# Holding a tile's pre-norm root and scalings behind the next tile's post-norm sums, at the seam of two layers

## The chip, the core and the metric

The kernel runs on one core of a Trainium2 chip. The metric is device time in microseconds of one execution; lower is better. Engines: PE (TensorE, matmuls), DVE (VectorE), ACT (ScalarE), POOL (GpSimd) and SP (SyncE, which here issues the DMAs). Each engine works through its own instructions in a fixed order and waits where an operand, or a buffer to write to, isn't ready.

## What is computed

Two layers of a decoder on 512 tokens of width 1024, each with a normalisation before its projections and one behind them. Cut to what matters here:

```python
def rms_norm(x, g):
    y = xf * lax.rsqrt(jnp.mean(xf * xf, axis=-1, keepdims=True) + NORM_EPS)
    return y * g

def hybrid_layer(x, w_in, w_out, g_pre, g_post, lb, g_head, sinks):
    h = rms_norm(x, g_pre)
    proj = jnp.einsum('bsd,de->bse', h, w_in)
    ...
    y = jnp.einsum('bse,ed->bsd', jnp.concatenate([o_h, o_a], axis=-1), w_out)
    return x + rms_norm(y, g_post)
```

The seam is the end of layer 0 and the start of layer 1: the last output projection, the post-norm with its residual, the pre-norm of layer 1, and layer 1's first projection (keys and values).

## The kernel before

Tokens are worked in four tiles of 128 (t0 to t3), each with two column halves of 512. To keep fp32 accuracy an operand is split into a high and a low part (`whi`, `wlo` for weights, `hhi`, `hlo` for the normalised input), and a product is three matmuls: high by high, high by low, low by high.

A projection is a queue of units (`Unit`); each unit is one output tile in one of three PSUM banks `pj`, and two units at most are worked at a time, in alternation. `step` issues the three matmuls of one k-slice (L293), then runs what `later` has put off by a number of steps, then converts weights that fall due (L181 on ACT, L182 on DVE or POOL). A weight piece may not be converted past `state["limit"]`, which the seam sets for the first slab of the next layer and lifts after the last tile's pre-norm.

At the seam the following happens for each tile t, all called from `final` as the output units end:

- the unit's result is added to `y` (L887, DVE, reads `pj`), half by half, and each half is squared with its sum (L929, ACT, into `ss`);
- the first half is multiplied by the post-norm gain on POOL (L931), the second on DVE (L936);
- post-norm root: the sum of the two halves (L352, DVE) and the power -0.5 (L354, POOL);
- residual: x plus the scaled y, half by half (L943, DVE, tile `a`, loaded by L920 into one of two buffers), stored to `x_mid` (L944, SP);
- `pre_norm`: squares of the new x (L386, ACT), pre-norm root (again L352 and L354), and the scalings to `xn`, half by half (L401, DVE; their gain lies in PSUM banks `ac`);
- put off by `DEFER` steps, for each half: four transposes into one of three PSUM banks `sc` (L406, PE), the high part (L410, ACT) and the low part (L414, DVE). The low part is the last reader of its `sc` bank.

The units of layer 1's key and value projection need the high and low parts of their tile. They are 24 matmuls of 128x256 each: eight high by high, eight high by low weight, eight low by high.

What stands where on an engine is decided by a scheduler of the language, which is free to move an instruction ahead of others; instructions given to `pin` keep the order in which the program issues them among themselves. In the kernel before, none of the DVE instructions of `final` and of `pre_norm` is pinned.

Of the kernel before, what the change touches and what calls it, by code (L numbers as in the profile page):

```python
# [14 lines left out]
ALU = mybir.AluOpType  # L15
# [5 lines left out]
NT = SEQ // 128  # L21
# [8 lines left out]
QA, IV, FQ, ZA, ZH = 0, 2, 4, 8, 10  # L30
# [10 lines left out]
DEFER = 18  # L41
# [29 lines left out]
def hybrid_kernel(ctx: ExitStack, tc: tile.TileContext, x, wkv, win, wout, g_pre, g_post, lbp, ghead, sinks,  # L71
                  gcol_c, cos_f, sin_f, cos_t, sin_t, masks_c, out):
    nc = tc.nc
# [10 lines left out]
    def pin(ins):  # L84
        return tc.keep_in_program_order(ins)
# [12 lines left out]
    def ac():  # L98
        ac_turn[0] += 1
        return ac_tiles[ac_turn[0] % len(ac_tiles)]  # L100

    def tmp(tag, dt=F32, n=1):

        t = tp.tile([P, n, 512] if n > 1 else [P, 512], dt, tag=tag, name=tag, bufs=TB[tag])
        return t
# [10 lines left out]
    slab_first = {}  # L116
# [37 lines left out]
    state = {"raw": 0, "conv": 0, "limit": KT // 2}  # L154
# [47 lines left out]
    def later(steps, key, fn):  # L202

        waiting.append([steps, key, fn])
# [131 lines left out]
    hT = {}  # L336
# [12 lines left out]
    def rstd2(ss, keep=lambda ins: ins):  # L349

        t = sm.tile([P, 1], F32, tag="s1", name="s1")
        keep(nc.vector.scalar_tensor_tensor(t, ss[:, 0:1], EPS, ss[:, 1:2], op0=ALU.add, op1=ALU.add))  # L352
        r = sm.tile([P, 1], F32, tag="r1", name="r1")
        keep(nc.gpsimd.tensor_tensor(r, t, mhalf[:, 0:1], op=ALU.pow))  # L354
        return r

    def halves(tag):
        t = tmp(tag, n=2)
        return [t[:, 0], t[:, 1]]

    def load_g(g):
        t = halves("b")
        for c in range(2):
            nc.sync.dma_start(t[c], g[c * 512:(c + 1) * 512].partition_broadcast(P))
        return t
# [54 lines left out]
            if self.tt == NT - 1 and c == 1:  # L420
                state["limit"] = None

    def pre_norm(tt, xt, g, hT, key, defer):
        m = Norm(tt, xt, g, hT)
        m.square(0)
        m.square(1)
        m.r = rstd2(m.ss)
        m.scale(0)
        m.scale(1)
        later(defer, None, lambda: m.rest(0))  # L430
        later(defer, key, lambda: m.rest(1))

    def new_hT():
        return (hp.tile([P, KT, SEQ], F32R, tag="hhi", name="hhi"), hp.tile([P, KT, SEQ], F32R, tag="hlo", name="hlo"))


    def layer(l, last):
# [440 lines left out]
        def wo_stream(b, s, final=None):  # L878
            def evac(o, tt, ch, c0, n):
                if (b, s) == ("a", 0):  # L880
                    if ch == 0:
                        yt[tt] = big.tile([P, 2, 512], F32, tag="oy", name="y", bufs=6)
                    nc.scalar.copy(yt[tt][:, ch], o)
                else:
                    y = yt[tt][:, ch, c0:c0 + n]
                    with tc.high_priority(200 if final else 0):
                        nc.vector.tensor_tensor(y, o, y, op=ALU.add)  # L887
                if final is not None:
                    final(tt, ch, c0, n)

            if final:
                todo = [(tt, ch, 0, 512) for tt in range(NT) for ch in range(2)]
                if last:

                    todo[-1:] = [(NT - 1, 1, 0, 256), (NT - 1, 1, 256, 256)]
            else:
                todo = [(tt, ch, 0, 512) for ch in range(2) for tt in range(NT)]
            enqueue(("out", l, f"{b}{s}"),
                    [(range(4 * ch, 4 * ch + 4), lambda k, w, tt=tt: tuple(t[:, k % 4, tt * P:(tt + 1) * P] for t in ops_t[b, s]),
                      lambda k, w, c0=c0, n=n: tuple(t[:, c0:c0 + n] for t in w[k]),  # L900
                      lambda o, e=(tt, ch, c0, n): evac(o, *e), [("o", l, b, s, tt)], n)
                     for tt, ch, c0, n in todo])


        hT2 = {}

        def final(tt, ch, c0, n):
            split = n < 512
            if ch == 0:
                if tt == 0:  # L910
                    hT2["gpost"] = load_g(g_post[l])
                    if not last:
                        hT2["gpre"] = [ac() for _ in range(2)]
                        for c, t in enumerate(load_g(g_pre[l + 1])):
                            nc.scalar.copy(hT2["gpre"][c], t)
                        state["limit"] = slab_first["in", l + 1, QA][0] + 2
                        hT[l + 1] = new_hT()
                hT2["x"] = halves("a")
                for c in range(2):
                    nc.sync.dma_start(hT2["x"][c], (x if l == 0 else x_mid)[tt * P:(tt + 1) * P, c * 512:(c + 1) * 512])  # L920
                hT2["ss"] = sm.tile([P, 2], F32, tag="ss", name="ss")
            xt, ss, y = hT2["x"], hT2["ss"], yt[tt]
            if c0:

                hT2["ss"] = sm.tile([P, 2], F32, tag="ss", name="ss")
                nc.vector.tensor_tensor(hT2["ss"][:, 0:1], ss[:, 0:1], ss[:, 1:2], op=ALU.add)
                ss = hT2["ss"]
            junk = tmp("u")
            nc.scalar.activation(junk[:, 0:n], y[:, ch, c0:c0 + n], AF.Square, scale=1.0 / 32.0, accum_out=ss[:, ch:ch + 1])  # L929
            if ch == 0:  # L930
                nc.gpsimd.tensor_tensor(y[:, 0], y[:, 0], hT2["gpost"][0], op=ALU.mult)  # L931
                return
            if not c0:
                hT2["yg"] = tmp("s")
            yg = hT2["yg"]
            nc.vector.tensor_tensor(yg[:, c0:c0 + n], y[:, 1, c0:c0 + n], hT2["gpost"][1][:, c0:c0 + n], op=ALU.mult)  # L936
            if split and not c0:
                return
            r = rstd2(ss)
            parts = [(0, y[:, 0], 0, 512)] + [(1, yg, e, n) for e in range(0, 512, n)]  # L940
            for i, (c, v, e, w) in enumerate(parts):
                xs = xt[c][:, e:e + w]
                nc.vector.scalar_tensor_tensor(xs, v[:, e:e + w], r, xs, op0=ALU.mult, op1=ALU.add)  # L943
                (nc.scalar if split and i == 1 else nc.sync).dma_start(  # L944
                    (out if last else x_mid)[tt * P:(tt + 1) * P, c * 512 + e:c * 512 + e + w], xs)
            if not last:
                pre_norm(tt, xt, hT2["gpre"], hT[l + 1], ("h", l + 1, tt), DEFER)


        for s_ in ORDER:  # L950
# [51 lines left out]
    gpre = [ac() for _ in range(2)]  # L1002
# [15 lines left out]
    m, n = head[0], head[1]  # L1018
# [146 lines left out]
```

## Time and profile before

| what | us |
|---|---|
| median of three runs | 923.82 |
| fastest, slowest of them | 923.78, 924.04 |
| span of the profiled execution (first to last instruction) | 921.4 |
| chain that ended last, PE's share of it | 88% |
| largest waits of PE in the seam (460 to 478) | 1.01, 1.01, 0.69 |

The profiled execution has no time of its own beside its span; the runs say what an execution takes as a whole. A row of the timeline gives start, duration, engine, line, operation, tile written <- tiles read, shape and count, and in brackets how long the engine stood idle ahead of it and who ended that. A row of the windows gives a stretch, its length, the busy time of PE, PE's weight loads, DVE, ACT and POOL (with counts), the granted clock of PE, the DMA engines' share and GB/s.

### The profile page before, as it was taken

The page shows a single profiled execution, that of the slowest core. Times are in us where ns is not written, and L with a number is a line of the kernel's source. Part 1 is how long each engine was busy: PE and PEld are TensorE (multiplying, and loading weights), DVE is VectorE, ACT ScalarE, POOL GpSimd, SP SyncE. Part 2 cuts the span into 40 slices and gives each one's busy share as a digit, 9 for nine tenths or more (in the row PEclk, how much of TensorE's full clock was granted, in tenths as well). Part 3 has the DMA queues.
Part 4 walks back from the last instruction along what each step waited for, and adds up shares of the span by engine and source line. Part 5 has one row for each costly group of instructions (what it writes and reads, how often), then busy time and mean ns, then how long its engine had stood idle before and what let it go on. Part 6 is the DMA issues. An engine that isn't in the chain of part 4 may idle for free.

```text
span 921.4 us, 19000 instructions
## 1 busy us (share of the span) xinstructions
PE 904.5 (98%) x7240; PEld 752.0 (82%) x7240; DVE 667.3 (72%) x1326; ACT 463.4 (50%) x1100; POOL 272.9 (30%) x292
## 2 busy tenths in 40 slices
PE   8999999999999999999989999999999999999996
PEld 7888887888888888888878878888788888888885
DVE  5967977869854896655786689876889449866556
ACT  6535767652755423534463366686446463245242
POOL 3325443304313142121332254450134022330102
PEclk9999999999999999999999999999999999999999
DMA  6684612333221432334356556222322323213413
GB/s 224 192 231 136 172 36 81 92 93 94 70 85 54 130 91 70 92 106 129 111 164 177 161 147 173 58 69 92 94 70 81 96 77 94 82 47 94 136 35 137
DMA packets 56570, 100.74 MB, mean 109 GB/s; under 512 B 6560, under 2 KB 9120, under 8 KB 56480
## 3 DMA queue, kind: packets, MB, share of 16 engines
q1 hardware_dynamic: 56192, 99.40, 36.6%
q8 instruction: 57, 0.93, 0.4%
q14 instruction: 33, 0.27, 0.1%
q10 hardware_dynamic: 288, 0.14, 0.1%
HBM read 86.93 MB, written 12.58 MB: 108 GB/s over the span
## 4 chain that ended last, share of the span: by engine, by line
PE 88%; DVE 6%; ACT 3%; issue 1%; POOL 1%; DMA 0%; POOLq 0%; DVEq 0%; ACTq 0%
PE pj L293 72%; PE sc L561 2%; PE sc L744 2%; PE ac L614 2%; PE ac L815 2%; DVE wlo L182 1%; PE ac L818 1%; PE ac L802 1%; PE sc L588 1%; ACT s L575 1%; PE sc L867 1%; PE sc L790 1%; POOL r L354 1%; DVE a L943 1%; PE sc L550 0%
## 5 line engine op out<-in xcount | busy, mean ns | idle before, releaser
L182 DVE TENSOR_TENSOR wlo<-raw,whi 128x512 fp32r<-128x512 f32 x249 | 182.9, 748 | 50.0 <-ACT whi L181 49.3
L181 ACT CAST whi<-raw 128x512 fp32r<-128x512 f32 x256 | 154.2, 620 | 106.0 <-PE pj L293 95.2
L293 PE MATMUL pj<-hhi,wlo 128*128 128x512 f32 x512 | 203.8, 398 | 0.0
L293 PE MATMUL pj<-hhi,whi 128*128 128x512 f32 x512 | 199.8, 390 | 0.0
L293 PE MATMUL pj<-hlo,whi 128*128 128x512 f32 x512 | 199.6, 390 | 0.0
L293 PE MATMUL pj<-whi,ops 128*128 128x512 f32 (+1 forms) x520 | 172.5, 394 | 0.0
L293 PEld LDWEIGHTS pj<-hhi,whi 128*128 128x128 f32 x512 | 96.1, 188 | 20.7
L293 PEld LDWEIGHTS pj<-whi,ops 128*128 128x128 f32 x520 | 97.2, 188 | 19.3
L293 PEld LDWEIGHTS pj<-hhi,wlo 128*128 128x128 f32 x512 | 96.1, 188 | 19.3
L293 PEld LDWEIGHTS pj<-hlo,whi 128*128 128x128 f32 x512 | 96.3, 188 | 18.6
L293 PE MATMUL pj<-whi,hlo 128*128 128x512 f32 x256 | 103.6, 405 | 0.0
L293 PE MATMUL pj<-wlo,ops 128*128 128x512 f32 (+1 forms) x260 | 100.8, 388 | 0.0
L293 PE MATMUL pj<-wlo,hhi 128*128 128x512 f32 x256 | 100.5, 392 | 0.3 <-DVE wlo L182 0.2
L293 PE MATMUL pj<-whi,hhi 128*128 128x512 f32 x256 | 100.3, 392 | 0.0
L763 POOL TENSOR_TENSOR k<-k,tot 128x256 f32<-128x256 f32 x80 | 64.2, 831 | 107.2 <-PE sc L744 57.7
L575 ACT ACTIVATE s<-sc,negm 128x128 f32<-128x128 f32 x128 | 45.5, 368 | 38.9 <-DVE negm L569 34.8
L762 DVE TENSOR_TENSOR q<-q,tot 128x256 f32<-128x256 f32 x80 | 48.8, 647 | 12.8 <-PE sc L750 7.0
L293 PEld LDWEIGHTS pj<-whi,hhi 128*128 128x128 f32 x256 | 48.1, 188 | 10.3
L293 PEld LDWEIGHTS pj<-wlo,ops 128*128 128x128 f32 x260 | 49.0, 188 | 8.8
L293 PEld LDWEIGHTS pj<-wlo,hhi 128*128 128x128 f32 x256 | 48.3, 189 | 9.1 <-DVE wlo L182 1.2
L293 PEld LDWEIGHTS pj<-whi,hlo 128*128 128x128 f32 x256 | 48.2, 188 | 8.0
L582 POOL TENSOR_TENSOR s<-s,sums 128x512 f32<-128x512 f32 x32 | 34.1, 1067 | 44.5 <-DVE sums L580 29.2
(188 smaller groups left out, 1416.2 us busy)
## 6 DMA issues: line engine op xcount, KB each, us to landing
raw<-in_win_dram SPq DMA_DIRECT2D x192, 256.0 KB, 2.7
raw<-in_wout_dram SPq DMA_DIRECT2D x64, 256.0 KB, 2.7
stack<-rot SPq DMA_DIRECT2D x16, 512.0 KB, 3.4
qs<-stack SPq DMA_DIRECT2D x32, 256.0 KB, 4.9
a<-in_x_dram SPq DMA_DIRECT2D x12, 256.0 KB, 3.0
raw<-in_wkv_dram SPq DMA_DIRECT2D x8, 256.0 KB, 4.2
x_mid<-a SPq DMA_DIRECT2D x8, 256.0 KB, 2.1
a<-x_mid SPq DMA_DIRECT2D x8, 256.0 KB, 3.2
```

Of the source, the lines that this page charges most:

```text
L181: keep(nc.scalar.copy(hi, v))
L182: keep((nc.gpsimd if i in on_pool and i % 2 else nc.vector).tensor_tensor(lo, v, hi.bitcast(F32), op=ALU.subtract))
L293: nc.tensor.matmul(u.o, lhsT=u.sta(k, u.w)[i], rhs=u.mov(k, u.w)[j], start=(n == 0), stop=(n == len(u.list) - 1))
L354: keep(nc.gpsimd.tensor_tensor(r, t, mhalf[:, 0:1], op=ALU.pow))
L561: pin(nc.tensor.matmul(S[:, h * 256:(h + 1) * 256], lhsT=q[:, 2 * hp_ + h, t_], rhs=kst[v][p][:, (n - 1) * P:(n + 1) * P], start=(h == 0 a ...
L575: nc.scalar.activation(pt[:, h * P:(h + 1) * P], cur[h], AF.Exp, bias=negm[:, h:h + 1], scale=SCALE, accum_out=sums[:, h:h + 1])
L582: nc.gpsimd.tensor_tensor(pv, pv, sums.unsqueeze(2).broadcast_to([P, 4, P]), op=ALU.mult)
L614: pin(nc.tensor.matmul(U, lhsT=vst[v][:, blk, :], rhs=d, start=(i == 0), stop=(i == len(terms) - 1)))
L744: pin(nc.tensor.matmul(L[32 * b:32 * b + 32, c:c + 16], lhsT=k[:, o_:o_ + 32], rhs=qv[:, blk:blk + qu, 1, :], start=True, stop=True, tile_ ...
L762: nc.vector.tensor_tensor(qv[:, :, 1, :], qv[:, :, 1, :], tv[:, :, 0].unsqueeze(2).broadcast_to([P, nb, hh]), op=ALU.mult)
L763: nc.gpsimd.tensor_tensor(kv_[:, :, 0, :], kv_[:, :, 0, :], tv[:, :, 1].unsqueeze(2).broadcast_to([P, nb, hh]), op=ALU.mult)
L815: pin(nc.tensor.matmul(O[:, c], lhsT=A[:, c], rhs=vs(j, n), start=(n == 0), stop=False))
```

## The change

`pre_norm` no longer issues the root and the scalings. It issues the squares and returns two functions, `root` and `scales`. `final` keeps them in `hT2["held"]` and calls them when the next tile has come to its own post-norm: `root` ahead of that tile's post-norm root, `scales` right behind it, with the transposes put off by `DEFER - 8` steps, counted from there. The last tile calls its own at once. Roots, scalings and residuals are pinned. The limit for early weight conversion falls from two pieces to one.

```diff
-    def pre_norm(tt, xt, g, hT, key, defer):
+    def pre_norm(tt, xt, g, hT, key):
         m = Norm(tt, xt, g, hT)
         m.square(0)
         m.square(1)
-        m.r = rstd2(m.ss)
-        m.scale(0)
-        m.scale(1)
-        later(defer, None, lambda: m.rest(0))
-        later(defer, key, lambda: m.rest(1))
+
+        def root():
+            m.r = rstd2(m.ss, pin)
+
+        def scales(defer):
+            for c in range(2):
+                pin(m.scale(c))
+            later(defer, None, lambda: m.rest(0))
+            later(defer, key, lambda: m.rest(1))
+
+        return root, scales
...
-                        state["limit"] = slab_first["in", l + 1, QA][0] + 2
+                        state["limit"] = slab_first["in", l + 1, QA][0] + 1
...
-            r = rstd2(ss)
+            held = hT2.pop("held", None)
+            if held:
+                held[0]()
+            r = rstd2(ss, pin if held else lambda ins: ins)
+            if held:
+                held[1](DEFER - 8)
             parts = [(0, y[:, 0], 0, 512)] + [(1, yg, e, n) for e in range(0, 512, n)]
             for i, (c, v, e, w) in enumerate(parts):
                 xs = xt[c][:, e:e + w]
-                nc.vector.scalar_tensor_tensor(xs, v[:, e:e + w], r, xs, op0=ALU.mult, op1=ALU.add)
+                (pin if not last else lambda ins: ins)(nc.vector.scalar_tensor_tensor(xs, v[:, e:e + w], r, xs, op0=ALU.mult, op1=ALU.add))
...
             if not last:
-                pre_norm(tt, xt, hT2["gpre"], hT[l + 1], ("h", l + 1, tt), DEFER)
+                hT2["held"] = pre_norm(tt, xt, hT2["gpre"], hT[l + 1], ("h", l + 1, tt))
+                if tt == NT - 1:
+                    root, scales = hT2.pop("held")
+                    root()
+                    scales(DEFER)
```

The lines behind the diff are numbered higher by 6 to 11 in the changed kernel: L887 becomes L893, L929 L935, L931 L937, L936 L942, L943 L954. What the scheduler makes of it is shown at three places. A row gives line, operation, tile written <- tiles read, and shape; the numbers tell buffers apart.

First place: DVE behind t0's residual (`a_5128`), where t1's second half is evicted. Before:

```order
L943 SCALAR_TENSOR_TENSOR a_5128<-s_5157,r1_5161,a_5128 128x512
L352 SCALAR_TENSOR_TENSOR s1_5171<-ss_5168 128x1
L887 TENSOR_TENSOR y_3077<-pj_5180,y_3077 128x512
L401 SCALAR_TENSOR_TENSOR xn_5167<-a_5128,r1_5173,ac1_82 128x512
L401 SCALAR_TENSOR_TENSOR xn_5167<-a_5128,r1_5173,ac0_81 128x512
L936 TENSOR_TENSOR s_5214<-y_3077,b_5118 128x512
L352 SCALAR_TENSOR_TENSOR s1_5216<-ss_5194 128x1
L887 TENSOR_TENSOR y_3126<-pj_5201,y_3126 128x512
```

With the change:

```order
L954 SCALAR_TENSOR_TENSOR a_5128<-s_5157,r1_5161,a_5128 128x512
L893 TENSOR_TENSOR y_3077<-pj_5174,y_3077 128x512
L942 TENSOR_TENSOR s_5208<-y_3077,b_5118 128x512
L352 SCALAR_TENSOR_TENSOR s1_5210<-ss_5168 128x1
L352 SCALAR_TENSOR_TENSOR s1_5214<-ss_5188 128x1
L401 SCALAR_TENSOR_TENSOR xn_5167<-a_5128,r1_5212,ac1_82 128x512
L401 SCALAR_TENSOR_TENSOR xn_5167<-a_5128,r1_5212,ac0_81 128x512
L893 TENSOR_TENSOR y_3126<-pj_5195,y_3126 128x512
```

t0's pre-norm sum (`ss_5168`) has moved behind t1's eviction and gain, and stands directly ahead of t1's post-norm sum; the scalings follow both.

Second place: DVE where t1's pre-norm (`ss_5225`, `xn_5224`), t2's residual (`a_5248`, then `a_5242`), t3's evictions (`y_3165`) and t0's low halves (`hlo`) meet. Before:

```order
L352 SCALAR_TENSOR_TENSOR s1_5228<-ss_5225 128x1
L936 TENSOR_TENSOR s_5271<-y_3126,b_5118 128x512
L401 SCALAR_TENSOR_TENSOR xn_5224<-a_5191,r1_5230,ac1_82 128x512
L401 SCALAR_TENSOR_TENSOR xn_5224<-a_5191,r1_5230,ac0_81 128x512
L352 SCALAR_TENSOR_TENSOR s1_5273<-ss_5251 128x1
L414 TENSOR_TENSOR hlo_5127<-sc0_78,hhi_5126 128x4x128
L943 SCALAR_TENSOR_TENSOR a_5248<-y_3126,r1_5275,a_5248 128x512
L887 TENSOR_TENSOR y_3165<-pj_5258,y_3165 128x512
L943 SCALAR_TENSOR_TENSOR a_5248<-s_5271,r1_5275,a_5248 128x512
L414 TENSOR_TENSOR hlo_5127<-sc1_79,hhi_5126 128x4x128
L887 TENSOR_TENSOR y_3165<-pj_5294,y_3165 128x512
```

With the change:

```order
L942 TENSOR_TENSOR s_5265<-y_3126,b_5118 128x512
L352 SCALAR_TENSOR_TENSOR s1_5267<-ss_5225 128x1
L352 SCALAR_TENSOR_TENSOR s1_5271<-ss_5245 128x1
L401 SCALAR_TENSOR_TENSOR xn_5224<-a_5185,r1_5269,ac1_82 128x512
L401 SCALAR_TENSOR_TENSOR xn_5224<-a_5185,r1_5269,ac0_81 128x512
L954 SCALAR_TENSOR_TENSOR a_5242<-y_3126,r1_5273,a_5242 128x512
L893 TENSOR_TENSOR y_3165<-pj_5252,y_3165 128x512
L954 SCALAR_TENSOR_TENSOR a_5242<-s_5265,r1_5273,a_5242 128x512
L414 TENSOR_TENSOR hlo_5127<-sc0_78,hhi_5126 128x4x128
L893 TENSOR_TENSOR y_3165<-pj_5288,y_3165 128x512
L414 TENSOR_TENSOR hlo_5127<-sc1_79,hhi_5126 128x4x128
```

The two sums stand together behind the gain, and t0's first low half has moved behind t2's residual and t3's first eviction.

Third place: PE in the key and value projection of t1 (`pj_5398`), with the transposes of t2 (`xn_5281`). Before:

```order
L293 MATMUL pj_5398<-wkv_4901,hhi_5126 128x256 x2
L293 MATMUL pj_5398<-wkv_4907,hhi_5126 128x256 x2
L293 MATMUL pj_5398<-wkv_4890,hhi_5126 128x256
L406 MATMUL sc1_79<-ident_106,xn_5281 128x128 x4
L406 MATMUL sc2_80<-ident_106,xn_5281 128x128 x4
L293 MATMUL pj_5398<-wkv_4890,hhi_5126 128x256
L293 MATMUL pj_5398<-wkv_4896,hhi_5126 128x256 x2
L293 MATMUL pj_5398<-wkv_4902,hhi_5126 128x256 x2
L293 MATMUL pj_5398<-wkv_4908,hhi_5126 128x256 x2
L293 MATMUL pj_5398<-wkv_4889,hlo_5127 128x256 x2
```

With the change:

```order
L293 MATMUL pj_5398<-wkv_4901,hhi_5126 128x256 x2
L406 MATMUL sc1_79<-ident_106,xn_5281 128x128 x4
L293 MATMUL pj_5398<-wkv_4907,hhi_5126 128x256 x2
L293 MATMUL pj_5398<-wkv_4890,hhi_5126 128x256 x2
L293 MATMUL pj_5398<-wkv_4896,hhi_5126 128x256 x2
L293 MATMUL pj_5398<-wkv_4902,hhi_5126 128x256 x2
L293 MATMUL pj_5398<-wkv_4908,hhi_5126 128x256 x2
L293 MATMUL pj_5442<-wkv_4889,hhi_5126 128x256
L406 MATMUL sc2_80<-ident_106,xn_5281 128x128 x4
L293 MATMUL pj_5398<-wkv_4889,hlo_5127 128x256 x2
```

The two groups of transposes are apart now, and one matmul of t2's own projection (`pj_5442`) stands between t1's high-part and low-part matmuls. On ACT two more weight casts (L181) stand ahead of t2's squares, and on SP the second x load of t3 stands behind the first store of t2; POOL's order is the same.

## The prediction

> **What bounds the kernel now.** I read the page first, then the windows around the seam, then each engine's timeline there.
>
> ```profile
> span 921.4 us, 19000 instructions
> PE 904.5 (98%) x7240; PEld 752.0 (82%) x7240; DVE 667.3 (72%) x1326; ACT 463.4 (50%) x1100; POOL 272.9 (30%) x292
> 463.50:478.00 14.50, 11.63 (x91) 10.73 (x91) 11.21 (x19) 8.12 (x19) 4.87 (x6) 1.00 0.40 121
> 478.00:500.00 22.00, 22.00 (x103) 18.27 (x102) 17.31 (x27) 9.91 (x18) 4.57 (x4) 1.00 0.51 163
> ```
>
> TensorE (PE) is busy for 98% of the span, so only a stretch in which it waits can be shortened. The seam is one: from 463.5 to 478 it is busy 11.63 of 14.50 us (second column), and right behind it 22.00 of 22.00. The granted clock is 1.00 in both. The PE rows of the seam follow (start, duration, line, tiles, in brackets the idle time ahead and who ended it).
>
> ```profile
> 448.47 0.61 PE L293 MATMUL pj<-whi,ops 128*128 128x512 f32 x2
> ...
> 455.50 1.03 PE L406 MATMUL sc<-ident,xn 128*128 128x128 f32 x8
> ...
> 459.82 1.24 PE L293 MATMUL pj<-wkv,hhi 128*128 128x256 f32 x9
> 460.89 1.04 PE L406 MATMUL sc<-ident,xn 128*128 128x128 f32 x8
> 461.68 1.07 PE L293 MATMUL pj<-wkv,hhi 128*128 128x256 f32 x7
> 462.59 1.12 PE L293 MATMUL pj<-wkv,hlo 128*128 128x256 f32 x8
> 464.72 1.34 PE L293 MATMUL pj<-wkv,hhi 128*128 128x256 f32 x9 [1.01 <-ACT hhi L410]
> ...
> 467.51 0.66 PE L406 MATMUL sc<-ident,xn 128*128 128x128 f32 x4 [1.01 <-DVE hlo L414]
> ...
> 471.90 0.66 PE L406 MATMUL sc<-ident,xn 128*128 128x128 f32 x4 [0.69 <-DVE xn L401]
> ...
> 476.89 1.12 PE L293 MATMUL pj<-wkv,hlo 128*128 128x256 f32 x8
> 477.85 0.40 PE L293 MATMUL pj<-hhi,wlo 128*128 128x512 f32 x1
> ```
>
> The k/v projection of layer 1 runs from 459.82 to 477.85, 18.03 us. Its 96 matmuls need 0.12 us each (eight from 476.89 to 477.85), its six groups of four transposes 0.40 each (eight from 460.89 to 461.68): 11.5 + 2.4 = 13.9. So 4.1 us are lost, more than the bracketed waits show, because a matmul's modelled tail counts as busy. **4.1 us is the ceiling of the gain.** Who is late is read from VectorE (DVE):
>
> ```profile
> 449.31 0.74 DVE L352 SCALAR_TENSOR_TENSOR s<-ss 128x1 f32<-128x1 f32 x1 [0.81 <-ACT hlo L386]
> ...
> 456.22 0.73 DVE L352 SCALAR_TENSOR_TENSOR s<-ss 128x1 f32<-128x1 f32 x1 [0.76 <-ACT hlo L386]
> 456.87 0.68 DVE L936 TENSOR_TENSOR s<-y,b 128x512 f32<-128x512 f32 x1
> 457.98 1.41 DVE L401 SCALAR_TENSOR_TENSOR xn<-a,r,ac 128x512 f32<-128x512 f32 x2 [0.44 <-POOL r L354]
> 459.31 0.15 DVE L352 SCALAR_TENSOR_TENSOR s<-ss 128x1 f32<-128x1 f32 x1
> 459.38 0.68 DVE L414 TENSOR_TENSOR hlo<-sc,hhi 128x512 fp32r<-128x512 f32 x1
> 460.17 0.75 DVE L943 SCALAR_TENSOR_TENSOR a<-y,r,a 128x512 f32<-128x512 f32 x1
> 460.84 0.68 DVE L887 TENSOR_TENSOR y<-pj,y 128x512 f32<-128x512 f32 x1
> 461.44 0.74 DVE L943 SCALAR_TENSOR_TENSOR a<-s,r,a 128x512 f32<-128x512 f32 x1
> 462.10 0.68 DVE L414 TENSOR_TENSOR hlo<-sc,hhi 128x512 fp32r<-128x512 f32 x1
> 462.70 0.68 DVE L887 TENSOR_TENSOR y<-pj,y 128x512 f32<-128x512 f32 x1
> ...
> 464.78 1.41 DVE L401 SCALAR_TENSOR_TENSOR xn<-a,r,ac 128x512 f32<-128x512 f32 x2 [0.44 <-POOL r L354]
> ...
> 470.21 0.16 DVE L352 SCALAR_TENSOR_TENSOR s<-ss 128x1 f32<-128x1 f32 x1
> 471.09 1.41 DVE L401 SCALAR_TENSOR_TENSOR xn<-a,r,ac 128x512 f32<-128x512 f32 x2 [0.72 <-POOL r L354]
> ```
>
> PE has left its last output unit at 459.82, but VectorE evicts it (L887) only at 462.70: VectorE is the late one. It stands still at a pre-norm root's sum (L352) for ScalarE's squares, and at the scalings (L401) for POOL's power. Its step is 0.60 us for a tensor_tensor (460.84 to 461.44), 0.665 for a 512-wide scalar_tensor_tensor (461.44 to 462.10), 0.07 for a root's sum (459.31 to 459.38). From 449.31 to the last scalings at 471.09 there are 14, 12 and 7 of these: 8.4 + 8.0 + 0.5 = 16.9 of 21.8 us. So VectorE waits 4.9 us there.
>
> ScalarE (ACT) and POOL rows of the same stretch, and one DVE row for the text on the port:
>
> ```profile
> 463.48 0.63 ACT L929 ACTIVATE u<-y 128x512 f32<-128x512 f32 x1 [0.52 <-DVE y L887]
> 464.10 1.05 ACT L410 CAST hhi<-sc 128x512 fp32r<-128x512 f32 x2
> 468.36 0.63 ACT L386 ACTIVATE hlo<-a 128x512 fp32r<-128x512 f32 x1 [2.93 <-DVE a L943]
> 468.99 0.56 ACT L410 CAST hhi<-sc 128x512 fp32r<-128x512 f32 x1
> ...
> 455.65 1.28 POOL L931 TENSOR_TENSOR y<-y,b 128x512 f32<-128x512 f32 x1 [2.24 <-ACT u L929]
> 457.02 0.93 POOL L354 TENSOR_TENSOR r<-s,mhalf 128x1 f32<-128x1 f32 x1
> ...
> 475.09 1.36 POOL L182 TENSOR_TENSOR wlo<-raw,whi 128x512 fp32r<-128x512 f32 x1 [4.04 <-ACT whi L181]
> 476.66 1.49 POOL L182 TENSOR_TENSOR wlo<-raw,whi 128x512 fp32r<-128x512 f32 x1 [0.20 <-ACT whi L181]
> ...
> 476.10 0.91 DVE L182 TENSOR_TENSOR wlo<-raw,whi 128x512 fp32r<-128x512 f32 x1 [0.80 <-ACT whi L181]
> ```
>
> **A price in these rows: POOL and VectorE block each other.** The sum at 456.22 takes 0.73 us instead of 0.15 and ends (456.95) with POOL's multiply (456.93); the one at 449.31 takes 0.74. POOL's power at 457.02 takes 0.93 instead of 0.55 and ends 0.40 behind VectorE's L936 (457.55). The wlo at 476.10 ends 0.56 behind POOL's (476.45), and POOL's next, begun in its time, ends 1.14 behind it. I use 0.02, 0.40, 0.56 and 1.14 as the ends of what gets blocked.
>
> The Trainium skill, page "SBUF — State Buffer", section "Who interferes with whom", states it as a rule: a VectorE instruction with two SBUF inputs contends with a GpSimd instruction that reads SBUF, and whoever issues first has the shared pair for the whole instruction. The rows above agree. It speaks against this change, which issues the multiply by the post-norm gain (L936) while POOL multiplies (L931): by the rule the sum is the one below, and without it some 1.0 us more would be gained.
>
> **The change, step by step** (estimates from the durations above; tiles t0 to t3). No instruction is added or removed; the order moves on four engines.
>
> *VectorE* ("now" marks a time of the trace of before). t1's second eviction no longer stands behind t0's root: its unit ends with the first of the two matmuls at 448.47, and even the second ends at 449.1 (448.47 + 0.61); I take 448.9. Its L936 follows at 449.6 and is blocked by L931 to 450.55, a loss of 0.3. Both sums, t0's pre-norm and t1's post-norm, then stand together, and POOL does both powers in one go (450.7, 451.3): one wait of 0.67 for two roots. t0's scalings start at 451.3, 0.6 later than now; their transposes come at 455.50. t2's L936 comes at 455.25; L931, ready at 455.45, waits for it and ends at 457.1, and holds t1's sum until then. That costs 0.9, about what the wait at 456.22 costs now. Then t1's scalings 457.75, t2's residual 459.1 (now 460.17), t3's evictions 459.75 and 461.6 (now 460.84 and 462.70), t2's scalings 464.65, t3's residual 466.0 (now 467.57), t3's scalings 469.5 (now 471.09). Waits fall from 4.9 to 3.75 us and the start is 0.4 earlier: 1.6 by the last scalings. What pays for it is t0's low half (L414), 461.0 instead of 459.38.
>
> *ScalarE.* The square of t3's second half (463.48 now) starts at 462.4, so t1's high half (L410) is ready at 463.6 instead of 464.67, as 464.10 plus 0.57. The two weight casts that move ahead of t2's squares lie in an idle stretch (458.0 to 459.1).
>
> *PE.* t1's second group of transposes writes the bank that t0's L414 must free. At present it is free in time; with the change PE waits from 461.3 to 461.75, a **new wait** of 0.45. The projection of t0 ends at 464.05 instead of 463.55, and t1's starts there instead of at 464.72. After six matmuls t2's first transposes wait for its scalings to 465.45. After ten more, a matmul of t2's projection, which the new order puts ahead of t1's low half, waits for t2's high half; that stands on ScalarE behind t3's square (the pair at 468.36 and 468.99; with the change 466.8 and 467.4, the cast done by 468.0): **468.05**. From there everything is ready in time: 56 matmuls and three groups of transposes, 6.7 + 1.2, and 0.1 for the restart: the first matmul of the next stage at 476.05, against 477.85. **Gain 1.8 us.**
>
> *SP.* The second x load of t3 is issued behind the first store of t2, so it waits for t2's residual (459.8) and lands by 465 even at 5.3 us; it is used at 466.65. Nothing.
>
> Bounds of what no row shows: were L931 not held up by L936, 0.35 more is gained; without any blocking, 1.0 more (2.75). Were two powers in a row to cost POOL 0.2 more each, 0.9 less. I take the blocking at full price, since three rows show it.
>
> **The rivals.** *More is gained*: L931 misses both L936, since a few tenths decide who comes first. 2.2 to 2.75 us, 921.1 to 921.6. For it: the margin at 455.25 against 455.45 is thin. Against it: the first contact has 1.1 us of overlap.
>
> *Given back later*: PE leaves the seam 1.8 earlier, but a stage behind it waits for something that keeps its own time. Then 923.4 to 923.9. Against it: the 22 us behind the seam hold no wait at all, and the weight casts and loads there are released by VectorE, which is earlier by as much. For it: the stretch in between has never run with less lead.
>
> *Slower*: t2's residual (L943) now heads a long row on VectorE (t3's evictions, both low halves of t0), and PE's transposes of t1 wait behind it in turn. It needs t2's x:
>
> ```profile
> 452.22 0.81 SPq L920 DMA_DIRECT2D a<-in_x_dram  x2
> DMA to landing us min/median/max: 2.6/3.1/5.3
> ```
>
> The load goes out when t0's scalings end, 0.3 to 0.6 later than now: 453, landed by 458.7 at the worst seen, used at 459.1. Each us beyond 459.1 costs a us; to come out 1.85 slower it would have to land at 462.7, about 926. Only a landing nearly twice as long as any here does that.
>
> **How the numbers follow.** The sum is made against the profiled execution's span; no total of that execution stands beside it, but the three runs (median 923.82) lie 2.4 to 2.6 us above it. What lies around the span I take as unchanged, so 923.82 - 1.8 = **922.0**. A measurement of this kernel can tell about 0.2% (1.85 us) from no change, and the forecast lies right at that bound: its own spread is 921.6 to 922.5. Chances: forecast 0.55 (0.25 beyond the bound, 0.30 within), more gained 0.20, given back 0.17, slower 0.08. So faster 0.45, same 0.47, slower 0.08. The range 921.0 to 923.6 leaves out the slower case and the edges of the others.
>
> **What would show it.** Right: t1's matmuls at about 4.2 us behind 459.82 instead of 4.9; a new wait of PE for L414 ahead of t1's second transposes; a wait for ScalarE's L410 of t2 as the last long one; L352 twice in a row with one wait behind; an L352 held to L931's end at t2. Wrong: L936 or L931 of usual length in spite of an overlap; t2's residual waiting for a DMA; PE waits between 478 and 500.

## The result, and the profile after

The changed kernel takes 921.37 us (median of 18 runs, 920.65 to 922.98); the kernel before, run beside it, 923.51 us (18 runs, 922.38 to 924.76). The ratio is 0.998, 95% interval 0.9973 to 0.9986: 1.3 to 2.5 us faster, 2.14 at the medians, or 0.23%. The forecast was 922.0, range 921.0 to 923.6.

The profiled execution of the changed kernel is its slowest, 922.98 us, and the page hardly differs from before:

```profile
span 921.3 us, 19004 instructions
PE 904.2 (98%) x7240; PEld 752.5 (82%) x7240; DVE 667.0 (72%) x1326; ACT 463.8 (50%) x1100; POOL 273.9 (30%) x292
```

So the spans of the two profiles (921.4 and 921.3) show no gain at all, and shares of busy time do not either. The reason is at the start. These are PE rows of the first microseconds, first of before, then of the changed kernel:

```profile
3.75 1.94 PE L1005 MATMUL ac<-ident,gcol 128*128 128x128 f32 x8
```

```profile
4.89 1.94 PE L1020 MATMUL ac<-ident,gcol 128*128 128x128 f32 x8 [1.28 <-DMA gcol<-in_gcol_dram]
```

PE waits 1.28 us for a load that was in time in the profile of before; further waits in the start-up follow, and at 20 us the changed execution is 2.44 us late, in code that the change does not touch. **The seam must therefore be measured by itself**: from the first matmul of layer 1's key and value projection to the first matmul of the next stage. The windows of it, of before and of the changed kernel (and the stretch behind it):

```profile
459.82:477.85 18.03, 15.16 (x121) 14.25 (x120) 14.78 (x25) 10.14 (x25) 6.11 (x7) 1.00 0.47 147
```

```profile
462.00:478.36 16.36, 14.80 (x121) 14.15 (x120) 13.80 (x25) 9.41 (x23) 5.71 (x6) 1.00 0.56 177
478.36:500.00 21.64, 21.64 (x102) 17.99 (x101) 16.90 (x27) 9.95 (x18) 4.53 (x4) 1.00 0.48 148
```

The same 121 PE records take 16.36 us in place of 18.03: **1.67 us gained**, where 1.8 was forecast. Behind the seam PE is busy without a gap in both. PE's rows in the changed seam:

```profile
462.00 1.24 PE L293 MATMUL pj<-wkv,hhi 128*128 128x256 f32 x9
...
463.98 0.66 PE L406 MATMUL sc<-ident,xn 128*128 128x128 f32 x4 [0.30 <-DVE hlo L414]
...
466.26 0.88 PE L293 MATMUL pj<-wkv,hhi 128*128 128x256 f32 x6
467.70 0.66 PE L406 MATMUL sc<-ident,xn 128*128 128x128 f32 x4 [0.56 <-DVE xn L401]
...
470.24 0.39 PE L293 MATMUL pj<-wkv,hhi 128*128 128x256 f32 x1 [0.70 <-ACT hhi L410]
470.46 0.60 PE L406 MATMUL sc<-ident,xn 128*128 128x128 f32 x4
470.82 1.20 PE L293 MATMUL pj<-wkv,hlo 128*128 128x256 f32 x8
471.86 0.88 PE L293 MATMUL pj<-wkv,hhi 128*128 128x256 f32 x6
...
478.36 0.40 PE L293 MATMUL pj<-hhi,wlo 128*128 128x512 f32 x1
```

The wait ahead of t1's matmuls (1.01 before) is gone: they start 4.26 us behind the first row (before 4.90). The new wait, ahead of t1's second transposes, is there (0.30), and the last long one is for ScalarE's high half of t2 (0.70). The other wait of 1.01 of before, ahead of t2's second transposes, is gone as well. VectorE and POOL in the same stretch:

```profile
451.81 0.97 DVE L942 TENSOR_TENSOR s<-y,b 128x512 f32<-128x512 f32 x1
452.70 0.21 DVE L352 SCALAR_TENSOR_TENSOR s<-ss 128x1 f32<-128x1 f32 x2
453.52 1.41 DVE L401 SCALAR_TENSOR_TENSOR xn<-a,r,ac 128x512 f32<-128x512 f32 x2 [0.60 <-POOL r L354]
...
457.48 0.69 DVE L942 TENSOR_TENSOR s<-y,b 128x512 f32<-128x512 f32 x1
458.20 1.21 DVE L352 SCALAR_TENSOR_TENSOR s<-ss 128x1 f32<-128x1 f32 x2
459.99 1.41 DVE L401 SCALAR_TENSOR_TENSOR xn<-a,r,ac 128x512 f32<-128x512 f32 x2 [0.58 <-POOL r L354]
461.31 0.75 DVE L954 SCALAR_TENSOR_TENSOR a<-y,r,a 128x512 f32<-128x512 f32 x1
```

```profile
450.93 1.30 POOL L937 TENSOR_TENSOR y<-y,b 128x512 f32<-128x512 f32 x1 [2.29 <-ACT u L935]
452.93 1.06 POOL L354 TENSOR_TENSOR r<-s,mhalf 128x1 f32<-128x1 f32 x2 [0.70 <-DVE s L352]
457.63 1.69 POOL L937 TENSOR_TENSOR y<-y,b 128x512 f32<-128x512 f32 x1 [3.64 <-ACT u L935]
...
465.93 1.43 POOL L354 TENSOR_TENSOR r<-s,mhalf 128x1 f32<-128x1 f32 x2 [1.09 <-DVE s L352]
```

Two sums stand together, POOL does two powers in one go, and VectorE waits once for both. The blocking is in the same rows: t1's gain (451.81) takes 0.97, since POOL's multiply runs until 452.23; t2's multiply (457.63) comes up 0.15 behind the start of VectorE's gain (457.48), takes 1.69 and ends 1.15 behind the gain's end, and the two sums at 458.20 take 1.21 in place of 0.21: they end 0.09 behind the multiply (459.32).

### The profile page after: what moved, and what is told of

Its sections match the earlier page's. It is cut to its first block, busy times and chain, and to the rows that moved or that the text cites. A ratio compares the mean times of both kernels' runs of the same rounds, so it can differ in the third digit from the quotient of the medians.

```text
span 921.3 us, 19004 instructions
## 1 busy us (share of the span) xinstructions
PE 904.2 (98%) x7240; PEld 752.5 (82%) x7240; DVE 667.0 (72%) x1326; ACT 463.8 (50%) x1100; POOL 273.9 (30%) x292
## 4 chain that ended last, share of the span: by engine, by line
PE 89%; DVE 6%; ACT 2%; issue 1%; POOL 1%; DMA 0%; POOLq 0%; DVEq 0%; ACTq 0%
PE pj L293 73%; PE sc L567 2%; PE ac L620 2%; PE sc L750 2%; PE ac L821 2%; DVE wlo L182 1%; PE ac L824 1%; PE ac L808 1%; PE sc L594 1%; ACT s L581 1%; PE sc L873 1%; PE sc L406 1%; PE sc L796 1%; DVE a L954 0%; PE sc L556 0%
## 5 line engine op out<-in xcount | busy, mean ns | idle before, releaser
L182 DVE TENSOR_TENSOR wlo<-raw,whi 128x512 fp32r<-128x512 f32 x249 | 182.8, 748 | 49.5 <-ACT whi L181 48.8
L181 ACT CAST whi<-raw 128x512 fp32r<-128x512 f32 x256 | 154.1, 620 | 105.9 <-PE pj L293 95.1
```

Of the source, the lines that this page charges most:

```text
L181: keep(nc.scalar.copy(hi, v))
L182: keep((nc.gpsimd if i in on_pool and i % 2 else nc.vector).tensor_tensor(lo, v, hi.bitcast(F32), op=ALU.subtract))
```

## The experiments

**The measure.** Matched matmul by matmul, each profile has an offset against the profile of before. The table gives it in us at five places; the seam's gain is the difference of the third and the second column, and equals the difference in seam length. The median is that of the kernel's own comparison; since the kernel before stood between 923.5 and 924.3 in these, the ratios count.

| kernel | at 20 us | at 450 | at 480 | at 540 | last matmul | seam, us | median, us |
|---|---|---|---|---|---|---|---|
| before | 0 | 0 | 0 | 0 | 0 | 18.03 | 923.51 |
| changed | 2.44 | 2.19 | 0.51 | 0.23 | -0.12 | 16.36 | 921.37 |
| e1_limit2 | 0.39 | 1.12 | -0.56 | -0.88 | -0.47 | 16.35 | 921.45 |
| e2_no_hold | 1.38 | 2.31 | 2.16 | 1.85 | 2.25 | 17.88 | 923.81 |
| e3_no_pin | -0.11 | -0.29 | -1.66 | -1.97 | -2.43 | 16.66 | 922.06 |
| e4_piece2 | 0.30 | -0.03 | -1.74 | -2.02 | -2.07 | 16.32 | 921.93 |
| e5_no_l937 | 1.11 | 0.63 | -2.24 | -2.57 | -2.76 | 15.14 | 920.39 |
| e6_sq_late | 0.82 | 1.11 | -1.18 | -1.50 | -1.34 | 15.74 | 921.03 |
| e7_sq_late_d9 | 1.14 | 1.86 | -1.00 | -1.03 | -1.19 | 15.17 | 921.63 |
| e8_changed | 1.81 | 1.39 | -0.28 | -0.57 | -0.94 | 16.38 | 921.80 |
| e9_sq_late_d9 | 0.45 | 0.68 | -2.23 | -2.28 | -2.48 | 15.13 | 920.61 |
| e10_sq_late_d9 | 0.41 | 0.20 | -2.69 | -2.71 | -3.13 | 15.15 | 921.57 |
| e11_changed | 1.31 | 1.74 | 0.08 | -0.21 | -0.20 | 16.37 | 920.99 |

### Which part of the change pays: limit, hold or pins

The limit alone undone:

```diff
-                        state["limit"] = slab_first["in", l + 1, QA][0] + 1
+                        state["limit"] = slab_first["in", l + 1, QA][0] + 2
```

> The changed kernel with the limit for early weight conversion at two pieces again, as before; everything else stays changed. On ACT two weight casts (L181) go back from ahead of t2's squares to behind t1's high halves (L410); DVE, PE, POOL and SP keep the changed order row for row. Theory (the hold makes the gain): in the changed kernel these casts stood in ACT's idle stretch (they run from 460.15, and ACT stands still 0.79 us behind them), and at the place they go back to ACT stands still 2.17 us for 1.15 us of casts. So the seam, from the first matmul of layer 1's key and value projection to the first matmul with the next low weights, stays at 16.4 +- 0.2 us (before 18.0, changed 16.4), and the time stays near 921.4. Rival (the earlier casts pay): the seam goes back towards 18.0, by at least 0.5 us.

Measured: seam 16.35 us, time 921.45 us, ratio 0.9981 (0.9972 to 0.9989). The limit neither pays nor costs anything that can be seen.

The hold alone undone, pins and limit kept (the put-off of the transposes goes back with it, from `DEFER - 8` to `DEFER`; t1's transposes stay behind the same nine matmuls, of t2's two groups the first comes three matmuls later and the second eight earlier):

```diff
-                if tt == NT - 1:
+                if True:
                     root, scales = hT2.pop("held")
                     root()
                     scales(DEFER)
```

> The changed kernel without the hold: every tile calls its own root and scalings at once, as before, while roots, scalings and residuals stay pinned and the limit stays at one piece. Theory (the hold makes the gain): each pre-norm sum stands ahead of the next tile's gain again, VectorE waits for ScalarE's squares and then for POOL's power apart, and the seam is 18.0 to 18.4 us, the time 923.3 to 924.0, as before the change. Rival (a fixed order on VectorE, or the limit, makes the gain): the seam stays near 16.4 and the time near 921.4.

Measured: 923.81 us, ratio 1.0003 (0.9994 to 1.0011), seam 17.88 (just under the 18.0 expected). **Without the hold 0.15 us is left in the seam, and nothing in the time.** VectorE at t2's scalings, t3's gain, its post-norm sum, t1's first low half and t3's residual:

```profile
467.09 1.41 DVE L401 SCALAR_TENSOR_TENSOR xn<-a,r,ac 128x512 f32<-128x512 f32 x2 [0.43 <-POOL r L354]
468.41 0.68 DVE L942 TENSOR_TENSOR s<-y,b 128x512 f32<-128x512 f32 x1
469.01 0.15 DVE L352 SCALAR_TENSOR_TENSOR s<-ss 128x1 f32<-128x1 f32 x1
469.08 0.68 DVE L414 TENSOR_TENSOR hlo<-sc,hhi 128x512 fp32r<-128x512 f32 x1
469.88 0.75 DVE L954 SCALAR_TENSOR_TENSOR a<-y,r,a 128x512 f32<-128x512 f32 x1
```

The scalings wait for the power of t2's own sum, the gain and the post-norm sum stand behind both scalings, and only then can POOL begin the next power; a low half fills most of that second wait.

The hold kept, nothing pinned (four edits like these two):

```diff
-            m.r = rstd2(m.ss, pin)
+            m.r = rstd2(m.ss)
...
-                pin(m.scale(c))
+                m.scale(c)
```

> The changed kernel with the hold, but nothing pinned. On VectorE each tile's pre-norm sum then stands ahead of the next tile's second eviction or gain, and the scheduler spreads other work between sums and scalings: one 512-wide operation between the two sums, one scaling between gain and post-norm sum. Theory (the hold makes the gain since it puts work of the next tile behind the sum while POOL works; that the two sums touch is not needed): VectorE again waits 0.9 us for ScalarE's squares at two sums, as before, but hardly for POOL any more (0.5 once, then under 0.2), so the scalings come as early as in the changed kernel; seam 16.4 to 16.7 us, time 921.4 to 921.8. Rival (the two sums behind one another, with one wait for two roots, are what pays, and that takes the pins): seam 17.2 to 18.0.

Measured: seam 16.66 us, at the upper end of what the theory gave; 922.06 us, ratio 0.9984 (0.9975 to 0.9993), above the 921.4 to 921.8 expected, though the interval takes that in. VectorE at t1's pre-norm, then the same place as above:

```profile
455.78 0.73 DVE L352 SCALAR_TENSOR_TENSOR s<-ss 128x1 f32<-128x1 f32 x1 [0.76 <-ACT hlo L386]
...
457.55 0.75 DVE L401 SCALAR_TENSOR_TENSOR xn<-a,r,ac 128x512 f32<-128x512 f32 x1 [0.44 <-POOL r L354]
...
463.83 0.68 DVE L942 TENSOR_TENSOR s<-y,b 128x512 f32<-128x512 f32 x1
464.44 0.15 DVE L352 SCALAR_TENSOR_TENSOR s<-ss 128x1 f32<-128x1 f32 x1
464.50 1.39 DVE L401 SCALAR_TENSOR_TENSOR xn<-a,r,ac 128x512 f32<-128x512 f32 x2
465.82 0.74 DVE L954 SCALAR_TENSOR_TENSOR a<-y,r,a 128x512 f32<-128x512 f32 x1
```

At t1's pre-norm VectorE stands still for the squares and for POOL as in the kernel before. At t2's it does not: a weight's low part, t3's gain and its post-norm sum stand ahead of the scalings, so the scalings wait for nothing, and the next power runs beside them, so the residual waits for nothing either. Counted with the prediction's step times (0.60, 0.665 and 0.07 us), VectorE waits as follows, by the tile whose pre-norm it is at; the four stretches run from t0's pre-norm sum to t3's first scaling. In the changed kernel the first three begin earlier in the row, with t1's second eviction and with t2's and t3's gain, which stand ahead of the sums there; it also begins 0.41 us earlier against the seam.

| kernel | t0 | t1 | t2 | t3 | all, us |
|---|---|---|---|---|---|
| before | 1.71 | 1.28 | 1.11 | 0.81 | 4.91 |
| e2_no_hold | 1.71 | 1.29 | 1.10 | 0.53 | 4.63 |
| e3_no_pin | 1.57 | 1.23 | 0.43 | 0.22 | 3.45 |
| changed | 1.20 | 1.75 | 0.61 | 0.22 | 3.78 |

So 1.37 of the 1.67 us remain without the two sums touching. **At t2, work of the next tile and its post-norm sum go out ahead of the held scalings: they fill one wait for POOL, and the scalings hide the next** (0.68 of the 1.46 us that VectorE saves without pins). At t3, whose root nothing holds, it is t2's first low half that now stands in the wait (0.59). What each of the two is worth in the seam was not tried apart, nor the put-off of the transposes by itself. With the pins the seam is 0.30 shorter; which of the pinned instructions that takes is open too.

### What a stretched power on POOL costs

In the changed kernel a weight's low part (L182) on VectorE stretches POOL's two powers, for t2's pre-norm and t3's post-norm, from 1.06 to 1.43 us (465.93). This kernel moves that weight piece out of the seam:

```diff
-        in_turn.update(slab_first["in", l, QA][0] + j for j in range(2, KT))
+        in_turn.update(slab_first["in", l, QA][0] + j for j in range(1, KT))
```

> The changed kernel with one weight piece more converted in turn instead of by due time: its cast (L181) leaves ACT's part between t1's squares and t0's high halves, and its low part (L182) leaves VectorE's wait for t2's two roots, where in the changed kernel it stretched POOL's two powers (1.43 us for two, against 1.06 for t0's two). VectorE puts a low half of t1 there instead. Theory (PE is held by the chain of t2 and t3 through ScalarE, not by these powers): t2's scalings come 0.4 us earlier, t3's scalings become late instead, since t3's sum now stands behind two low halves, and the seam is 16.2 to 16.5 us: no change. Rival (the stretched powers are on the path): all of 0.4 to 0.9 us is gained, seam 15.5 to 16.0, and this version beats both.

Measured: seam 16.32 us, 921.93 us, ratio 0.9982 (0.9973 to 0.9991). POOL's pair and the wait of PE behind it:

```profile
463.71 1.05 POOL L354 TENSOR_TENSOR r<-s,mhalf 128x1 f32<-128x1 f32 x2 [1.09 <-DVE s L352]
```

```profile
469.93 1.31 PE L406 MATMUL sc<-ident,xn 128*128 128x128 f32 x8 [0.66 <-DVE xn L401]
```

The powers are short again; beside them stands a low half (463.62), which reads one input from PSUM. Seen from the first row of the seam, t2's scalings come 0.39 earlier than in the changed kernel (4.50 against 4.89), and so do t3's (9.34 against 9.73). Yet the seam is the same to 0.04: PE, which no longer waits for t2's high half, waits for t3's scalings instead, and those wait 0.72 for POOL. It isn't that t3's sum stands behind two low halves, as expected, since it does so in the changed kernel too (469.54); there, t2's first low half fills the wait behind that sum (470.92); here it stands ahead of the sum, since t1's first has moved into t2's wait (463.62). t2 and t3 are two chains of nearly equal length. What the stretch would be worth with the low halves left in their places, this edit does not show.

### What the blocking of POOL and VectorE costs

This kernel leaves out POOL's multiply in layer 0, so it computes something else and serves to measure alone:

```diff
-                nc.gpsimd.tensor_tensor(y[:, 0], y[:, 0], hT2["gpost"][0], op=ALU.mult)
+                if last:
+                    nc.gpsimd.tensor_tensor(y[:, 0], y[:, 0], hT2["gpost"][0], op=ALU.mult)
```

> The changed kernel without POOL's multiply by the first half of the post-norm gain (L937) in layer 0; that half of the post-norm of layer 0 goes unscaled. Every other instruction of every engine keeps its place. It asks what the overlap of POOL's multiply with VectorE's (L942) costs, which the prediction charged at full price. Theory (each blocks the other): without it t1's gain takes 0.68 in place of 0.97, t2's two sums 0.2 in place of 1.21, so t1's scalings come 1.2 us earlier, t2's and t3's as well, and the wait for t0's low half goes; the seam is 15.2 +- 0.3 us (changed 16.4), the time 920.0 to 920.6. Rival (they run side by side, and the long sum waits for something else): the long sum stays at 1.2, seam 16.2 to 16.4.

Measured: seam 15.14 us (15.2 expected), 920.39 us, ratio 0.9967 (0.9955 to 0.998). VectorE at t1's and t2's gain (in this kernel line L943), the sums and the scalings:

```profile
450.25 0.69 DVE L943 TENSOR_TENSOR s<-y,b 128x512 f32<-128x512 f32 x1
...
456.37 0.16 DVE L352 SCALAR_TENSOR_TENSOR s<-ss 128x1 f32<-128x1 f32 x1
456.98 0.16 DVE L352 SCALAR_TENSOR_TENSOR s<-ss 128x1 f32<-128x1 f32 x1 [0.46 <-ACT u L935]
457.18 1.41 DVE L401 SCALAR_TENSOR_TENSOR xn<-a,r,ac 128x512 f32<-128x512 f32 x2
```

The gain takes 0.69 again and the sums 0.16 each, the second of them behind a wait for ScalarE's square (0.46). t1's scalings come 3.26 ahead of the first row of the seam, in place of 2.01. So POOL's multiply, by its overlap with VectorE at two tiles, costs the changed seam 1.2 us (16.36 - 15.14), nearly three quarters of what the change gained.

### Is there an order without it

The multiply of t2 comes late because t2's first square stands behind the first square of t1's new x on ScalarE. Here, on top of e4_piece2, the pre-norm squares are held as well, until the next tile's first square and multiply are issued (the last tile calls its own at once; cut here):

```diff
-        m.square(0)
-        m.square(1)
+        def squares():
+            return m.square(0), m.square(1)
...
                 nc.gpsimd.tensor_tensor(y[:, 0], y[:, 0], hT2["gpost"][0], op=ALU.mult)
-                return
+                return "held" in hT2 and hT2["held"][2]()
```

> The kernel of e4_piece2 (one piece more in turn), in which also the squares of a tile's new x (L386) are held, until the next tile's first square (L935) and POOL's multiply (L937) are issued. On ACT t2's and t3's first squares move ahead of the pair of squares of the tile before; VectorE keeps its order up to t3's second eviction, where one low half of t0 and then one of t1 change places with an eviction and with t2's scalings. Theory (the multiply on POOL comes too late and holds t2's sums): the multiply of t2 starts 1.2 us earlier, so that t2's two sums run at 0.2 instead of 1.2 and t1's scalings come 1.0 us earlier; then PE waits about 1 us for t1's first low half ahead of t2's second transposes, which takes back some; seam 15.5 to 15.9 us, time 920.4 to 921.0. Rival (the earlier multiply only meets VectorE's residual of t1, which reads two SBUF tiles as well, and one blocks the other there): the residual or the multiply is stretched to 1.3 or more, the scalings gain less than 0.4, seam 16.0 to 16.4.

Measured: seam 15.74 us, 921.03 us, ratio 0.9969 (0.9957 to 0.998). VectorE, then POOL, then PE:

```profile
455.03 0.74 DVE L954 SCALAR_TENSOR_TENSOR a<-s,r,a 128x512 f32<-128x512 f32 x1
455.69 0.68 DVE L893 TENSOR_TENSOR y<-pj,y 128x512 f32<-128x512 f32 x1
456.41 1.07 DVE L942 TENSOR_TENSOR s<-y,b 128x512 f32<-128x512 f32 x1
457.40 0.22 DVE L352 SCALAR_TENSOR_TENSOR s<-ss 128x1 f32<-128x1 f32 x2
```

```profile
455.35 1.59 POOL L937 TENSOR_TENSOR y<-y,b 128x512 f32<-128x512 f32 x1 [2.43 <-ACT u L935]
```

```profile
468.24 0.66 PE L406 MATMUL sc<-ident,xn 128*128 128x128 f32 x4 [0.98 <-DVE hlo L414]
```

Part of the rival came true and did not decide. The multiply does meet t1's residual: it ends at 456.94, 1.17 behind the residual's end (455.77), the price read off other rows in the prediction being 1.14. But the eviction between (455.69), which reads PSUM and one SBUF tile, takes its usual 0.68, and the gain ends 0.54 behind the multiply (predicted 0.56), so the two sums take 0.22. t1's scalings come 0.7 us earlier (2.72 ahead of the first row of the seam, against 2.01), where 1.0 was expected, and the time is just above the 920.4 to 921.0. By the rule of the Trainium skill, page "SBUF — State Buffer", section "Who interferes with whom", a VectorE instruction with two SBUF inputs contends with a GpSimd instruction that reads SBUF, and one with at most one SBUF input, outside its two-port modes, does not; the residual, the gain and the eviction of this trace agree. What is late next is, as expected, t1's first low half (0.98).

One step less of put-off moves that low half ahead:

```diff
-                held[1](DEFER - 8)
+                held[1](DEFER - 9)
```

> The kernel of e6_sq_late with the transposes put off by one step less (DEFER - 9): the transposes stand three matmuls earlier on PE, and t1's first low half stands between the two sums of t2's pre-norm and t3's post-norm on VectorE, in the wait for POOL. Theory: the wait of about 1 us for that low half goes; no wait of PE in the seam is above 0.5 us, and layer 1's next stage starts 2.9 to 3.3 us earlier than in the kernel before (against 1.7 in the changed kernel), time 920.0 to 920.6: faster than both. Rival as for e6_sq_late: about 2.0 or less.

Measured: seam 15.17 us, a gain of 2.86, a hair under the 2.9 to 3.3 expected; 921.63 us, ratio 0.997 (0.9957 to 0.9982), which misses the 920.0 to 920.6. One wait of PE is left in the seam:

```profile
466.40 1.31 PE L406 MATMUL sc<-ident,xn 128*128 128x128 f32 x8 [0.30 <-DVE xn L401]
```

So the trace says 1.2 us better than the changed kernel, and the median 0.26 worse; but that median is of another comparison, in which the kernel before stood 0.64 higher too, and the intervals of the two ratios overlap (0.9957 to 0.9982, and 0.9973 to 0.9986). Is the gain given back behind the seam, or is it lost in scatter? The two kernels were run beside each other twice more, unchanged.

> The changed kernel itself once more, beside e9_sq_late_d9 on one chip, to set the two against each other. Theory: seam 16.4 us, ratio to before 0.9977 to 0.9985, and less than a third of the difference between single executions comes from the seam: the rest is there before the seam is reached (up to 2.5 us by 20 us into the span).

> The kernel of e7_sq_late_d9 once more, beside the changed kernel. Theory (the time follows the seam): the seam gains 2.9 us again, 1.2 more than the changed kernel, so the median is 0.8 to 1.6 us below that of e8_changed. Rival (what the seam gains is given back behind it): the medians are within 0.3.

Measured: 921.80 against 920.61 us; ratios to before 0.9978 (0.9969 to 0.9986) and 0.9965 (0.9951 to 0.9979); seams 16.38 and 15.13, all as the theory had it. The two profiles of the changed kernel differ by 0.02 us in the seam, and by 0.63 us at 20 us.

> The kernel of e7_sq_late_d9 a third time, beside the changed kernel: its seam gains 1.2 us more than the changed kernel's in each profile, its medians so far were 921.63 and 920.61 against 921.37 and 921.80. Theory (the time follows the seam): over all runs of the two kernels the medians come to stand 0.6 to 1.4 apart. Rival (given back behind the seam): under 0.4.

> The changed kernel a third time, beside e10_sq_late_d9; seam 16.4 us, median 921.4 to 921.8.

Measured: 921.57 against 920.99 us, the other way round; ratios 0.997 (0.9958 to 0.9982) and 0.9968 (0.9956 to 0.9981); seams 15.15 and 16.37 (461.56 to 477.93). The changed kernel's median is below the 921.4 to 921.8 expected.

Over all runs the changed kernel stands at 921.56 us (median of 34) and this one at 920.99 (median of 17); the means differ by 0.46 us. That lies between what the theory (0.6 to 1.4) and the rival (under 0.4) gave, and of the two comparisons side by side one has this kernel 1.19 lower, the other 0.58 higher. That the **time** of an execution is shorter is not shown by the clock. The profiles say why it is hard to see: the start, where no edit stands, scatters by more. From 450 us to the last matmul the three changed profiles gain 2.31, 2.33 and 1.94 us against before, the three of this kernel 3.05, 3.16 and 3.33. So behind the start this kernel is some 1.0 us shorter in every profile. In the seam it is 1.2; between 480 and 540 part is given back: the changed profiles gain 0.28, 0.29 and 0.29 more there, the three of this kernel 0.03, 0.05 and 0.02. What takes it back is open.

## Why the prediction was right

**The place: right.** All of the gain that the profiles tie to the change lies in the seam, and the 22 us behind it run without a gap as before. The ceiling of 4.1 us was 0.2 too high, by the price of the transposes below.

**The steps on VectorE and PE: right to 0.1 us.** The changed seam begins 2.18 us later than before (462.00 against 459.82); with that taken off, forecast and trace stand like this:

| step | forecast | trace less 2.18 |
|---|---|---|
| t1's gain, held by POOL's multiply, ends | 450.55 | 450.60 |
| t0's scalings | 451.3 | 451.34 |
| POOL's multiply of t2 ends | 457.1 | 457.14 |
| t1's scalings | 457.75 | 457.81 |
| t2's residual | 459.1 | 459.13 |
| t1's second transposes on PE, behind the new wait | 461.75 | 461.80 |
| t1's matmuls on PE | 464.05 | 464.08 |
| t2's first transposes on PE | 465.45 | 465.52 |
| the matmul of t2's projection on PE | 468.05 | 468.06 |
| next stage | 476.05 | 476.18 |

**The price of the blocking: right.** Charged at full price for the gain of t1 and the sums of t2, it stands in the rows, and e5_no_l937 gives what it costs in all, 1.2 us. The forecast put 1.0 on it. The rival by which more is gained needed the multiply to miss the gain at both tiles. At t2 it met it by 0.15 us (457.48 against 457.63), a margin as thin as forecast. At t1 the prediction spoke of 1.1 us of overlap, which its rows do not give: 449.6 for the gain against the multiply's end at 450.03 in the profile of before is 0.4, and the trace has 0.42 (451.81 to 452.23).

**The size: 0.13 us off, in the last term.** From the last wait to the next stage the sum had 56 matmuls at 0.12, three groups of transposes at 0.40 and 0.1 for a restart, 8.0 us; the trace has 8.12 (470.24 to 478.36). It is the groups of transposes that were mis-sized. Four take 0.36 to the next matmul (470.46 to 470.82), but the matmul behind them takes 0.20 in place of 0.12, in each of the five such groups of the changed seam that are followed by a matmul. That is why the eight matmuls at 470.82 take 1.04 (to 471.86) where eight elsewhere take 0.96 (476.89 to 477.85 in the rows of before). So a group costs 0.44; the 0.40 was half of eight in a row (460.89 to 461.68), with the slow matmul behind them left out. Three times 0.04 is the 0.12.

**Why it gained: half right.** The prediction gave "one wait of 0.67 for two roots" as the reason, and that is how the changed kernel does it. e3_no_pin shows that most of the gain does not need it: 1.37 of 1.67 us remain with the sums apart. And the table of waits shows that the joint wait paid at t0 and t2 (0.5 us each), while at t1 the blocking took back as much; at t3, which has no pair, another 0.6 came from a low half in the wait. The prediction's sum had all of this (waits from 4.9 to 3.75 us, measured 3.78), its sentence on the reason only the first.

**Against the clock.** The forecast was 1.8 us from a median of three runs, 923.82; the 18 runs beside the changed kernel have 923.51, and the measured difference is 2.14. The seam accounts for 1.67. Of the rest the profiles give no cause that belongs to the change: the changed profile gains 0.28 between 480 and 540, but so does e2_no_hold (0.31), which gained 0.15 in the seam, and behind 540 the kernels' offsets go 0.46 down (e3_no_pin) or 0.41 up (e1_limit2). 1.67 lies inside the interval of 1.3 to 2.5. It also lies below the 1.85 us that the prediction took as the least to be told from no change; the interval turned out narrower than that, and no change lies outside it.

**The rivals.** *Given back later* did not happen to the changed kernel. *Slower*, by a late load of t2's x: the residual at 461.31 follows the scalings without a wait.

## What to carry to other kernels

Where two chains of different tiles go through the same slow hand-over (here VectorE to POOL and back), issue the second chain's request before taking the first one's answer: the first one's work then hides the second one's wait. The wait for the first answer wants other work in it, as the low half at t3 shows. Before moving an instruction, see which other engine it will run beside: here a multiply on POOL and one on VectorE cost 1.2 us by blocking each other, and the seam got as much back when a weight piece, ScalarE's squares and the transposes were put in another order (e7_sq_late_d9). And where a change is worth less than the scatter of the start, compare the stage, matched instruction by instruction, and not the span.

## What the runs showed of the hardware that was not expected

- **The start scatters more than the change is worth.** The thirteen profiles reach the seam between 459.53 us (e3_no_pin) and 462.13 us (e2_no_hold), 2.6 us apart. At 20 us, where these kernels have done the same work, they lie between 0.11 ahead of the profile of before and 2.44 behind it; one source is the wait for `gcol`, which was none before and 1.28 us in the changed profile. The seams of four profiles with the same order on PE (changed, e1_limit2, e8_changed, e11_changed) lie between 16.35 and 16.38.
- **A residual blocks POOL as well.** The 128x512 scalar_tensor_tensor on two SBUF tiles (e6_sq_late, 455.03) held POOL's multiply up by as much as a tensor_tensor does (1.17 against 1.14 us beyond its end). The prediction's rows had tensor_tensor alone for that.
- **The first matmul behind a group of transposes is slower.** It takes 0.20 us to the next one (0.200 to 0.203, five times in the changed seam), all other matmuls of that shape that run without a wait 0.12. Why is not known.
